# Alternating the small matmuls of an RWKV-7 recurrence over halves of the TensorE array

## The chip, the cores and the metric

The program runs on one core of a Trainium2 chip. The metric is the device time of one execution in microseconds, the median of several runs. Engines are named as the profile names them: PE is TensorE's matmul stream, PEld its weight loads, DVE is VectorE, ACT is ScalarE, POOL is GpSimd, SP is the queue that issues the weight transfers.

## The reference

One layer of a streaming encoder trunk for 256 prompt and 64 sample tokens with the same weights (320 token columns, worked on together):

```python
h = rmsnorm(x, norm_mix)
u_pool, u_rw, g_pool, g_rw = split(h @ w_in)
y_a, new_pool = pool_mixer(u_pool, ...)               # windows 2/4/8/16
y_b, new_shift, S = rwkv7_mix(u_rw, ...)              # 16 heads x 64
merged = sigmoid(g_pool) * (y_a @ proj_pool) + sigmoid(g_rw) * (y_b @ proj_rwkv)
x = x + merged @ w_out
x = x + (silu(h2 @ w_ffn_gate) * (h2 @ w_ffn_up)) @ w_ffn_down
x = x + sigmoid(h3 @ w_ple_gate) * (p @ w_ple_proj)
# inside rwkv7_mix, per token and head:
sa = S @ (-kk_t)
S = S * w_t + outer(sa, b_t) + outer(v_t, k_t)
y = S @ r_t
```

Everything is computed in float32 to float32 accuracy.

## The kernel before

The big products (gemm, L104; mm3, L107) hold features on partitions and stream the 320 token columns. Each weight block is split into a head and a rest in float32r (ACT makes the head, L93; DVE the rest, L56), so a 128 x 128 block costs three matmuls of 320 columns (L110 to L112). There are 11,984 of them in the program, here called gemm matmuls; they accumulate in the two PSUM buffers of tag acc.

The RWKV part works on four groups of four heads (group(g)), with two feature tiles jj of two heads h each. The tokens are cut into five chunks of 64: chunk 4 is the sample, 0 to 3 the prompt. The recurrence is done by chunks, with plain float32 matmuls, each of which stands in the trace as two instructions:

- the decay and in-context rates, tile z: a product with 128 rows (L441), then one with the rest in 64 rows only (L442);
- masked products within a chunk, tiles g0 and g4 (g in the trace, L510 and L513): 64 rows, 128 columns out, 128 moving columns, 20 per group; all of one head half h, then all of the other, because a head half lies on partitions 0 to 63 or 64 to 127;
- two rounds of 32 x 32 products per group for a triangular inverse, pz and px (L569, L574);
- for each chunk in the order 4, 0, 1, 2, 3: a read of the state and of the masked products, ry (L594, L599); an ACT copy, rhs (L603); the solve, pu (L606); an ACT copy, uv (L607); the new state, ps_s (L613), added and scaled by eight small DVE operations on 64 x 64 blocks (L621, L622); the chunk's output, py_c (L628). Chunk 0 starts from no state, chunk 4 from the given one, chunks 1 to 3 from the chunk before.

The order on each engine is made by a scheduler that simulates the program; gemm matmuls of later tiles (the projections of the next group, then as many gate tiles as FILLS says, 5, 4, 4 and 22) are put between the dependent small products. PE takes its instructions in that order. The small products share two PSUM tags of three buffers each:

```python
psB = ctx.enter_context(tc.tile_pool(name="psB", bufs=3, space=PSUM))   # L72
def small(name, shape, tag="pk"):                                       # L82
    return psB.tile(shape, F32, tag=tag, name=name)
```

Of the kernel before, what the change touches and what calls it, by code (L numbers as in the profile page):

```python
# [18 lines left out]
P = 128  # L19
# [20 lines left out]
# columns of the per-feature table  # L40
# [8 lines left out]
def trunk_step(ctx: ExitStack, tc: tile.TileContext, xT, pT, cols, w_low, s0T, poolpast, cst, maskc, invc,  # L49
# [22 lines left out]
    psB = ctx.enter_context(tc.tile_pool(name="psB", bufs=3, space=PSUM))  # L72
# [9 lines left out]
    def small(name, shape, tag="pk"):  # L82
        return psB.tile(shape, F32, tag=tag, name=name)

# [13 lines left out]
    def gemm(acc, src, ks, name, xs, k0=0, first=True, last=True, un=8):  # L98
        """acc += W[k0:k0+ks].T @ x, xs(k) -> (head, rest)"""
# [26 lines left out]
    def rsqrt(pl, v, eps, shape, tag, bufs, out):  # L126
        """out = 1/sqrt(v + eps), with one Newton step"""
# [26 lines left out]
    def shift(q, rp, t, out):  # L154
        """token shift of the projected tile in rp[:, :, 1:]"""
# [6 lines left out]
    # pooling inputs and gates go to DRAM until both branches are projected  # L162
# [20 lines left out]
    # x * g goes to the tensor engine, 1 / rms scales what comes out  # L183
    with tc.tile_pool(name="start", bufs=1) as st:
# [38 lines left out]
        def pp_mm(m0, n, u):  # L223
            h, l = u
            for i in range(n):
                a = small("acc_pp", [P, NT])
# [42 lines left out]
        def narrow(acc, src):  # L269
            """the last low-rank columns come four times: three heads and, in the last rows, the weights' rest"""  # L270
# [39 lines left out]
        zl = rf.tile([P, NT], F32R, name="zl")  # L310
        z_in = []
        for i in range(2):
            lo, hi = slice(64 * i, 64 * i + 64), slice(64 - 64 * i, 128 - 64 * i)
            h = rf.tile([P, NT], F32R, name=f"z{i}")
            act.copy(h[lo], t0[lo])
            act.copy(h[hi], t0[lo])
            TT(zl[lo], t0[lo], f(h[lo]), ALU.subtract)
            z_in.append((lo, h))
# [24 lines left out]
    def pool_diff(gi, z):  # L343
        """trailing means minus the token, split"""
# [22 lines left out]
    def pool_mix(gi, dh, dl):  # L367
        h, l = unit(w_poolw[gi], 4, f"pw{gi}")
        for i in range(2):
            j = 2 * gi + i  # L370
            a = small("acc_pw", [P, NT], "pf")
# [12 lines left out]
    d_gs = dr.tile([8, P, NT], F32, name="d_gs")  # L384
    d_yb = dr.tile([8, P, NT], F32, name="d_yb")
    with tc.tile_pool(name="rk", bufs=1) as rk:

        def shift_tile(q, out):
            """one projected tile with its token shift, into out [P, NT]"""
# [26 lines left out]
        def group(g):  # L416
# [6 lines left out]
            # low-rank paths: decay rate, in-context rate, output gate  # L423
# [20 lines left out]
            go = tp("go")  # L444
            for jj in range(2):
                b = slice((4 + jj) * P, (5 + jj) * P)
                z = small("pg", [P, NT], "pf")
                pe.matmul(out=z, lhsT=lw[:, b], rhs=t1h, start=True, stop=False)
                pe.matmul(out=z, lhsT=lw[:, b], rhs=t1l, start=False, stop=False)
                pe.matmul(out=z, lhsT=lwl[:, jj * P:(jj + 1) * P], rhs=t1h, start=False, stop=False)  # L450
                pe.matmul(out=z, lhsT=lw[0:96, (6 + jj) * P:(7 + jj) * P], rhs=t2s[0:96], start=False, stop=True)
                act.copy(go[:, jj, :], z)
# [12 lines left out]
            # key directions  # L465
# [7 lines left out]
            sqh, sql = split_tp(sq)  # L473
            for jj in range(2):
                s = small("s_kk", [P, NT], "pf")
                head_sum(s, sqh[:, jj, :], sql[:, jj, :])
                vec.tensor_scalar(out=am[:, jj, :], in0=s, scalar1=1e-24, scalar2=None, op0=ALU.max)
# [14 lines left out]
            # r.k bonus  # L492
# [3 lines left out]
            kfh, kfl = split_tp(kf)  # L496
            for jj in range(2):
                s = small("s_rk", [P, NT], "pf")
                head_sum(s, kfh[:, jj, :], kfl[:, jj, :])
                mul(bv[:, jj, :], s, xv[:, jj, :])  # L500
            # masked products within each chunk; rows (b s | k s), columns (a t | r t)
            mg = rk.tile([P, 4, NCH, P], F32, tag="mg", name="mg", bufs=2)
            gm = gmask.unsqueeze(1)
            for h in range(2):
                lo = slice(64 * h, 64 * h + 64)
                g4 = small("g4", [P, 2, P], "pf")
                for jj in range(2):
                    g0 = small("g0", [P, 4, P], "pf")
                    for c in range(4):
                        pe.matmul(out=g0[:, c, :], lhsT=bk[lo, jj, c].rearrange("p s t -> p (s t)"),  # L510
                                  rhs=ar[lo, jj, c].rearrange("p s t -> p (s t)"), start=True, stop=True)
                    mul(mg[:, 2 * jj + h, 0:4, :], g0, gm.broadcast_to([P, 4, P]))
                    pe.matmul(out=g4[:, jj, :], lhsT=bk[lo, jj, 4].rearrange("p s t -> p (s t)"),  # L513
                              rhs=ar[lo, jj, 4].rearrange("p s t -> p (s t)"), start=True, stop=True)
                mul(mg[:, h::2, 4, :], g4, gm.broadcast_to([P, 2, P]))
# [4 lines left out]
            for u0 in range(0, 10, 4):  # L520
                n = min(4, 10 - u0)
                pb = small("pb", [P, n, P], "pf")
# [5 lines left out]
            pv = small("pv", [P, 2, 2, P], "pf")  # L528
            for s in range(2):
                for jj in range(2):  # L530
                    pe.transpose(out=pv[:, s, jj, :], in_=xv[:, jj, s * P:(s + 1) * P], identity=ident)
            pv4 = small("pv4", [64, 2, P], "pf")
            for jj in range(2):
                pe.transpose(out=pv4[:, jj, :], in_=xv[:, jj, 256:320], identity=ident)
            uvf = uv.rearrange("p c h v -> p c (h v)")
            for h in range(2):
                act.copy(uvf[64:128, h:4:2, :], pv[64 * h:64 * h + 64].rearrange("p s j v -> p s (j v)"))
            act.copy(uvf[64:128, 4, :], pv4.rearrange("p j v -> p (j v)"))
            # X = (I - F)^-1, F strictly upper: diagonal blocks by substitution, one block per partition
# [19 lines left out]
            X = rk.tile([64, 20, 64], F32, tag="X", name="X")  # L559
            tz = rk.tile([64, 20, 32], F32, tag="tzz", name="tzz")  # L560
            pool.memset(X[32:64, :, 0:32], 0.0)
            for b in range(2):
                lo = slice(32 * b, 32 * b + 32)
                pool.dma_start(out=X[lo, :, lo], in_=dX[b].rearrange("u s t -> s u t"))
            pool.dma_start(out=tz[0:32], in_=dT.rearrange("u t s -> t u s"))
            for u0 in (0, 10):
                pz = small("pz", [64, 10, 32])
                for u in range(10):
                    pe.matmul(out=pz[32:64, u, :], lhsT=mgu[0:32, u0 + u, 32:64], rhs=tz[0:32, u0 + u, :],  # L569
                              start=True, stop=True)  # L570
                act.copy(tz[32:64, u0:u0 + 10, :], pz[32:64])
                px = small("px", [32, 10, 32])
                for u in range(10):
                    pe.matmul(out=px[:, u, :], lhsT=tz[32:64, u0 + u, :], rhs=X[32:64, u0 + u, 32:64],  # L574
                              start=True, stop=True)
                act.copy(X[0:32, u0:u0 + 10, 32:64], px)
            # chunk recurrence
            ysb = rk.tile([P, 3, 4, C], F32, tag="ysb", name="ysb")
            pool.memset(ysb[64:128, 2], 0.0)
            sbd_in = rk.tile([P, 2, P], F32, tag="sbd", name="sbd_in", bufs=3)  # L580
# [4 lines left out]
            sbd = None  # L585
            for c in (4, 0, 1, 2, 3):
                if c == 4:
                    cur = sbd_in
                elif c == 0:
                    cur = None  # L590
                ry = small("ry", [P, 4, C])
                if cur is not None:
                    for jj in range(2):
                        pe.matmul(out=ry[:, 2 * jj:2 * jj + 2, :].rearrange("p h v -> p (h v)"),  # L594
# [328 lines left out]
```

## Time and profile before

| | |
|---|---|
| median of 3 runs | 1930.12 us (1928.15 to 1931.4) |
| profiled execution, first to last instruction | 1928.3 us |
| PE busy | 1906.9 us, 99% |
| DVE, ACT, POOL busy | 59%, 42%, 7% |
| DMA | 302.98 MB, mean 157 GB/s |

The profile gives no time for the profiled execution other than its span; the median of the runs is 1.8 us above that. Durations of matmul records overlap: a record lasts longer than the distance to the next one, so costs on PE are read from start to start.

### The profile page before, as it was taken

What the parts mean: (1) busy time and instruction counts of PE and PEld (TensorE: products, weight loads), DVE (VectorE), ACT (ScalarE), POOL (GpSimd) and SP (SyncE); (2) the same over time, 40 slices, a digit from 0 to 9 for tenths busy, and PEclk for the clock granted to TensorE, in tenths of its full rate; (3) what the DMA queues carried; (4) which work ended last, traced back from release to release, by engine and by line L of the source; (5) the groups of instructions that cost most, each with busy time, mean ns of one, the idle gap of its engine ahead of it and who ended that gap; (6) DMA issues with size and microseconds to landing.
All of it is one profiled execution on the core that took longest, in us unless ns stands there. A gap on an engine that the chain in (4) does not pass through costs nothing.

```text
span 1928.3 us, 32558 instructions
## 1 busy us (share of the span) xinstructions
PE 1906.9 (99%) x13304; PEld 1873.3 (97%) x13304; DVE 1139.0 (59%) x1764; ACT 803.6 (42%) x1072; POOL 134.7 (7%) x274
## 2 busy tenths in 40 slices
PE   8999999999999999999999999999999999999997
PEld 7999999999999999999999999999999999999997
DVE  7577785788767666555554554444455455444665
ACT  6545436455355334444333333333333333333443
POOL 0101112111031113000000000000000000000000
PEclk9999999999999999999999999999999999999998
DMA  8444444345345566444444444555444444555453
GB/s 280 165 155 154 141 134 150 112 139 189 124 147 178 173 202 233 161 149 149 148 152 152 147 151 144 149 150 158 148 149 153 150 147 149 151 150 151 159 172 119
DMA packets 95221, 302.98 MB, mean 157 GB/s; under 512 B 12096, under 2 KB 23248, under 8 KB 95072
## 3 DMA queue, kind: packets, MB, share of 16 engines
q1 hardware_dynamic: 78336, 271.71, 43.7%
q0 software_dynamic: 6688, 17.39, 3.1%
q10 hardware_dynamic: 10048, 11.80, 1.7%
q8 instruction: 105, 1.72, 0.4%
q14 instruction: 44, 0.36, 0.1%
HBM read 284.12 MB, written 16.73 MB: 156 GB/s over the span
## 4 chain that ended last, share of the span: by engine, by line
PE 98%; DVE 1%; DMA 0%; issue 0%; ACT 0%; DVEq 0%
PE acc_fd L111 5%; PE acc_fg L110 5%; PE acc_fg L112 5%; PE acc_fu L112 5%; PE acc_fu L110 5%; PE acc_fu L111 5%; PE acc_fg L111 5%; PE acc_fd L112 5%; PE acc_fd L110 5%; PE acc_f L112 4%; PE acc_f L111 4%; PE acc_f L110 4%; PE acc_q L110 3%; PE acc_q L112 3%; PE acc_q L111 3%; PE acc_pg L110 2%
## 5 line engine op out<-in xcount | busy, mean ns | idle before, releaser
L111 PE MATMUL acc_fg<-nl,wh_fg 128*128 128x320 f32 x704 | 217.8, 309 | 0.0
L110 PE MATMUL acc_fg<-nh,wh_fg 128*128 128x320 f32 x704 | 217.6, 309 | 0.1
L110 PE MATMUL acc_fu<-nh,wh_fu 128*128 128x320 f32 x704 | 217.5, 309 | 0.0
L112 PE MATMUL acc_fu<-nh,wl_fu 128*128 128x320 f32 x704 | 217.5, 309 | 0.0
L111 PE MATMUL acc_fu<-nl,wh_fu 128*128 128x320 f32 x704 | 217.5, 309 | 0.0
L112 PE MATMUL acc_fg<-nh,wl_fg 128*128 128x320 f32 x704 | 217.5, 309 | 0.0
L56 DVE TENSOR_TENSOR wl_fd<-raw_fd,wh_fd 128x1024 fp32r<-128x1024 f32 (+1 forms) x96 | 109.1, 1136 | 151.7 <-ACT wh_fd L93 151.7
L93 ACT CAST wh_fd<-raw_fd 128x1024 fp32r<-128x1024 f32 (+1 forms) x96 | 94.1, 980 | 203.1 <-PE acc_fd L111 162.4
L93 ACT CAST wh_fg<-raw_fg 128x1024 fp32r<-128x1024 f32 x88 | 92.5, 1051 | 199.4 <-PE acc_fg L111 98.7
L93 ACT CAST wh_fu<-raw_fu 128x1024 fp32r<-128x1024 f32 x88 | 92.5, 1052 | 190.7 <-PE acc_fu L111 100.6
L56 DVE TENSOR_TENSOR wl_fg<-raw_fg,wh_fg 128x1024 fp32r<-128x1024 f32 x88 | 107.8, 1225 | 105.6 <-ACT wh_fg L93 105.6
L110 PE MATMUL acc_f<-xh,wh_f 128*128 128x320 f32 x512 | 160.4, 313 | 0.0
L111 PE MATMUL acc_f<-xl,wh_f 128*128 128x320 f32 x512 | 160.0, 313 | 0.0
L112 PE MATMUL acc_f<-xh,wl_f 128*128 128x320 f32 x512 | 159.8, 312 | 0.1
L110 PE MATMUL acc_fd<-hh,wh_fd 128*128 128x320 f32 x512 | 158.2, 309 | 0.0
L111 PE MATMUL acc_fd<-hl,wh_fd 128*128 128x320 f32 x512 | 158.2, 309 | 0.0
L112 PE MATMUL acc_fd<-hh,wl_fd 128*128 128x320 f32 x512 | 158.2, 309 | 0.0
L56 DVE TENSOR_TENSOR wl_fu<-raw_fu,wh_fu 128x1024 fp32r<-128x1024 f32 x88 | 107.8, 1225 | 83.9 <-ACT wh_fu L93 83.9
L110 PEld LDWEIGHTS acc_fg<-nh,wh_fg 128*128 128x128 f32 x704 | 132.1, 188 | 0.3 <-issue 0.3
L111 PEld LDWEIGHTS acc_fg<-nl,wh_fg 128*128 128x128 f32 x704 | 132.1, 188 | 0.1
L112 PEld LDWEIGHTS acc_fg<-nh,wl_fg 128*128 128x128 f32 x704 | 132.1, 188 | 0.1
L110 PEld LDWEIGHTS acc_fu<-nh,wh_fu 128*128 128x128 f32 x704 | 132.1, 188 | 0.0
(491 smaller groups left out, 5015.3 us busy)
## 6 DMA issues: line engine op xcount, KB each, us to landing
raw_fg<-in_w_gate SPq DMA_DIRECT2D x88, 512.0 KB, 3.7
raw_fu<-in_w_up SPq DMA_DIRECT2D x88, 512.0 KB, 3.8
raw_f<-in_w_in SPq DMA_DIRECT2D x64, 512.0 KB, 4.0
raw_fd<-in_w_down SPq DMA_DIRECT2D x64, 512.0 KB, 3.6
raw_q<-in_w_in SPq DMA_DIRECT2D x48, 512.0 KB, 4.0
raw_o<-in_w_out SPq DMA_DIRECT2D x32, 512.0 KB, 3.8
raw_pg<-in_w_pg SPq DMA_DIRECT2D x32, 512.0 KB, 3.8
raw_fd<-in_w_down SPq DMA_DIRECT2D x32, 384.0 KB, 3.6
```

The source lines that it names most:

```text
L56: return vec.tensor_tensor(out=out, in0=a, in1=b, op=op)
L93: act.copy(h, raw)
L110: pe.matmul(out=acc, lhsT=hs[i], rhs=xh, start=first and i == 0, stop=False)
L111: pe.matmul(out=acc, lhsT=hs[i], rhs=xl, start=False, stop=False)
L112: pe.matmul(out=acc, lhsT=ls[i], rhs=xh, start=False, stop=last and i == n - 1)
```

## The change

The small products are issued in alternation over two parts of the array. Masked products alternate between the row halves h, in two PSUM banks. The inverse's 32 x 32 products for jj = 0 and 1 go to different partitions and alternate. The recurrence keeps jj = 0 on partitions 0 to 63 and jj = 1 on 64 to 127: the read's left side is cut into its two 64-column halves, ra (before the solve) and py_c (after it, where the state is now read a second time), the solve alternates over row halves, and the new state over column halves. Chunks 4 and 0 go through these steps together, so that there are four steps per group and not five. The state update takes four DVE operations of double width. The 64-row product of z is padded with zeros to 128 rows. PSUM tags get one buffer each: s and cs of one bank, w and cw of two banks.

```diff
-    psB = ctx.enter_context(tc.tile_pool(name="psB", bufs=3, space=PSUM))
+    psB = ctx.enter_context(tc.tile_pool(name="psB", bufs=1, space=PSUM))
-    def small(name, shape, tag="pk"):
+    def small(name, shape, tag="s"):
         return psB.tile(shape, F32, tag=tag, name=name)
+    def wide(name, parts=P, tag="w"):
+        return psB.tile([parts, 2, 512], F32, tag=tag, name=name)
...
-                a = small(f"acc_t{q}", [P, NT], "pf")
+                a = small(f"acc_t{q}", [P, NT], ("", "s", "cs")[q])
...
+            zl = rf.tile([P, NT], F32R, name=f"zl{i}")
+            vec.memset(f(zl[hi]), 0.0)
...
-                lo, h = z_in[i]
+                z = wide("z")
                 for jj in range(2):
                     w = lw[:, (2 * i + jj) * P:(2 * i + jj + 1) * P]
-                    z = small("z", [P, NT], "pf")
-                    pe.matmul(out=z, lhsT=w, rhs=h, start=True, stop=False)
-                    pe.matmul(out=z, lhsT=w[lo], rhs=zl[lo], start=False, stop=True)
-                    act.activation(o[:, jj, :], z, AF.Sigmoid, bias=col(c + 2 * g + jj))
+                    for part in range(2):
+                        pe.matmul(out=z[:, jj, 0:NT], lhsT=w, rhs=z_in[i][part], start=part == 0, stop=part == 1)
...
-            for h in range(2):
-                lo = slice(64 * h, 64 * h + 64)
-                g4 = small("g4", [P, 2, P], "pf")
-                for jj in range(2):
-                    g0 = small("g0", [P, 4, P], "pf")
-                    for c in range(4):
-                        pe.matmul(out=g0[:, c, :], lhsT=bk[lo, jj, c]..., rhs=ar[lo, jj, c]..., start=True, stop=True)
+            for jj in range(2):
+                g0 = wide("g0")
+                for c in range(4):
+                    for h in range(2):
+                        product(g0[:, h, c * P:(c + 1) * P], h, jj, c)
...
+            for u in range(10):
+                for jj in range(2):
+                    pe.matmul(out=pz[64 * jj + 32:64 * jj + 64, u, :], lhsT=mgu[0:32, 10 * jj + u, 32:64],
+                              rhs=tz[0:32, 10 * jj + u, :], start=True, stop=True)
...
+            for u in range(10):
+                for jj in range(2):
+                    q = slice(64 * jj + 32, 64 * jj + 64)
+                    pe.matmul(out=px[64 * jj:64 * jj + 32, jj, 32 * u:32 * u + 32], lhsT=tz[q, u, :],
+                              rhs=X[q, u, 32:64], start=True, stop=True)
...
-            for c in (4, 0, 1, 2, 3):
...
+            def read(out, half, c, cur):
+                if cur is not None:
                     for jj in range(2):
+                        pe.matmul(out=out[halves[jj]]..., lhsT=ar[:, jj, c, half, :], rhs=cur[:, jj, :],
+                                  start=True, stop=False)
+                for h in range(2):
+                    for jj in range(2):
+                        pe.matmul(out=out[halves[jj], h, :], lhsT=mg[:, 2 * jj + h, c, halves[half]],
+                                  rhs=uv[:, c, 2 * jj + h, :], start=cur is None and h == 0, stop=h == 1)
+            for cs in ((4, 0), (1,), (2,), (3,)):
+                ra = small("ra", [P, n, 2, C], "cs")
+                for i, c in enumerate(cs):
+                    read(ra[:, i], 0, c, states[c])
+                act.copy(rhs, ra)
+                pu = wide("pu", 64, "cw")
+                for i, c in enumerate(cs):
                     for h in range(2):
+                        for jj in range(2):
+                            pe.matmul(out=pu[:, jj, q:q + C], lhsT=X[halves[jj], h * NCH + c, :],
+                                      rhs=rhs[halves[jj], i, h, :], start=True, stop=True)
...
+                for i, c in enumerate(cs):
+                    for jj in range(2):
+                        for h in range(2):
+                            pe.matmul(out=ps[halves[h], i, jj, :], lhsT=bt[:, jj * NCH + c, halves[h]],
+                                      rhs=uv[:, c, 2 * jj + h, :], start=True, stop=True)
...
+                    for lo in halves:
+                            TT(nxt[lo, :, lo], src, states[c][lo, :, lo], ALU.add)
+                        mul(nxt[lo, :, lo], src, pcs[lo, :, c:c + 1].broadcast_to([64, 2, C]))
...
+                for i, c in enumerate(cs):
+                    read(py[:, i], 1, c, states[c])
```

How the order on PE moves is seen in two places. The first is group 1, chunk 2, late in its recurrence. On PE, before, a read of the state (ry) was followed by masked products of group 2 (g) and by gemm matmuls (acc_f); five rows further on stands the solve pu:

```order
L594 MATMUL ry<-sbd,ar 128x128 x2
L599 MATMUL ry<-uv,mg 64x64 x3
L599 MATMUL ry<-uv,mg 128x64
L510 MATMUL g_3619<-ar,bk 128x128 x4
L110 MATMUL acc_f_5246<-xh,wh_f_0_5249 128x320
L111 MATMUL acc_f_5246<-xl,wh_f_0_5249 128x320
L112 MATMUL acc_f_5246<-xh,wl_f_0_5251 128x320
L110 MATMUL acc_f_5246<-xh,wh_f_0_5249 128x320
L513 MATMUL g_3618<-ar,bk 128x128 x2
```

In the change the same chunk stands on PE like this, with the last gemm matmul ahead of it and the next one behind it:

```order
L117 MATMUL acc_q_4485<-xh,wl_q_8_4520 128x320
L613 MATMUL ra<-sbd,ar 64x128 x2
L617 MATMUL ra<-uv,mg 64x64 x4
L633 MATMUL pu<-rhs,X 64x64 x4
L642 MATMUL ps_s<-uv,bt 64x64 x4
L613 MATMUL py_c<-sbd,ar 64x128 x2
L617 MATMUL py_c<-uv,mg 64x64 x4
L613 MATMUL ra<-sbd,ar 64x128 x2
L617 MATMUL ra<-uv,mg 64x64 x4
L417 MATMUL s_rk<-sp_h,bonesr 128x320
L115 MATMUL acc_q_4554<-xh,wh_q_0_4557 128x320
```

No gemm matmul is left between the read, the solve, the new state and the next chunk's read there. In most of the other steps 20 to 33 gemm matmuls stand between them, as before.

The second place is the masked products of group 0. On PE, before, they came in pieces:

```order
L510 MATMUL g_1120<-ar,bk 128x128 x4
L110 MATMUL acc_q_1873<-xh,wh_q_8_1906 128x320
L111 MATMUL acc_q_1873<-xl,wh_q_8_1906 128x320
L112 MATMUL acc_q_1873<-xh,wl_q_8_1908 128x320
L110 MATMUL acc_q_1873<-xh,wh_q_8_1906 128x320
L513 MATMUL g_1119<-ar,bk 128x128
L510 MATMUL g_1127<-ar,bk 128x128 x4
L513 MATMUL g_1119<-ar,bk 128x128
```

In the change the eight products of one jj stand together on PE, the two head halves in turn:

```order
L117 MATMUL acc_q_1915<-xh,wl_q_8_1950 128x320
L515 MATMUL g_1114<-ar,bk 128x128 x8
L115 MATMUL acc_q_1915<-xh,wh_q_8_1948 128x320
L116 MATMUL acc_q_1915<-xl,wh_q_8_1948 128x320
```

The next such eight follow 29 gemm matmuls later, and the four of chunk 4 another 29 later. Counted over the whole program's PE order, the part of the array that a matmul uses (its rows x columns) changes from one matmul to the next 245 times before and 141 times in the change.

## Rows read from the trace of the kernel before

**Rows 1.** The page: busy time by engine, and the chain that ended last.

```profile
PE 1906.9 (99%) x13304; PEld 1873.3 (97%) x13304; DVE 1139.0 (59%) x1764; ACT 803.6 (42%) x1072; POOL 134.7 (7%) x274
...
PE 98%; DVE 1%; DMA 0%; issue 0%; ACT 0%; DVEq 0%
```

**Rows 2.** Waits of PE (us in total, times, longest), first and last of eight.

```profile
PE acc_pp L110 <- ACT pp L231: 2.5, 3, 1.2
...
PE acc_pp L111 <- DVE pl__125 L56: 0.4, 1, 0.4
```

**Rows 3.** Timeline of PE around one solve: start us, duration us, then the instruction.

```profile
495.51 0.31 PE L110 MATMUL acc_f<-xh,wh_f 128*128 128x320 f32 x1
495.75 0.67 PE L606 MATMUL pu<-rhs,X 64*64 64x64 f32 x8
496.36 0.42 PE L111 MATMUL acc_f<-xl,wh_f 128*128 128x320 f32 x1
496.61 0.31 PE L112 MATMUL acc_f<-xh,wl_f 128*128 128x320 f32 x1
...
499.54 0.31 PE L111 MATMUL acc_f<-xl,wh_f 128*128 128x320 f32 x1
```

**Rows 4.** Timeline of PE around four masked products of one half.

```profile
133.49 0.31 PE L112 MATMUL acc_q<-xh,wl_q 128*128 128x320 f32 x1
133.72 1.16 PE L510 MATMUL g<-ar,bk 64*128 64x128 f32 x8
134.81 0.41 PE L110 MATMUL acc_q<-xh,wh_q 128*128 128x320 f32 x1
135.06 0.30 PE L111 MATMUL acc_q<-xl,wh_q 128*128 128x320 f32 x1
```

**Rows 5.** Groups of PE instructions by line and form: count, busy us, mean ns.

```profile
L510 PE MATMUL g<-ar,bk 64*128 64x128 f32 x128 | 17.4, 281 | 0.0
L606 PE MATMUL pu<-rhs,X 64*64 64x64 f32 x160 | 13.5, 224 | 0.1
```

**Rows 6.** Timeline of PE where products of two array parts meet.

```profile
226.49 0.72 PE L574 MATMUL px<-X,tzz 32*32 32x32 f32 x17
...
227.08 0.19 PE L569 MATMUL pz<-tzz,mg 32*32 32x32 f32 x1
227.08 0.19 PE L574 MATMUL px<-X,tzz 32*32 32x32 f32 x1
...
227.14 0.70 PE L569 MATMUL pz<-tzz,mg 32*32 32x32 f32 x17
...
228.99 0.27 PE L513 MATMUL g<-ar,bk 64*128 64x128 f32 x1
229.10 0.27 PE L510 MATMUL g<-ar,bk 64*128 64x128 f32 x1
229.10 0.27 PE L513 MATMUL g<-ar,bk 64*128 64x128 f32 x1
229.21 0.72 PE L510 MATMUL g<-ar,bk 64*128 64x128 f32 x5
```

**Rows 7.** Timeline of all engines at a hand-off through ACT, group 3.

```profile
586.13 0.59 PE L599 MATMUL ry<-uv,mg 128*64 128x64 f32 x3
...
586.75 0.37 ACT L603 COPY rhs<-ry 128x256 f32<-128x256 f32 x1 [0.49 <-PE ry L599]
...
587.18 0.33 PE L606 MATMUL pu<-rhs,X 64*64 64x64 f32 x2
```

**Rows 8.** The same at the new state's hand-off through DVE.

```profile
591.12 0.61 PE L613 MATMUL ps_s<-uv,bt 128*128 128x128 f32 x4
591.22 1.04 ACT L93 CAST wh_f<-raw_f 128x1024 fp32r<-128x1024 f32 x1 [2.27 <-issue]
591.59 0.98 DVE L56 TENSOR_TENSOR sbd<-ps_s,sbd_in 64x64 f32<-64x64 f32 x4 [1.80 <-PE ps_s L613]
...
593.54 0.82 DVE L622 TENSOR_SCALAR sbd<-sbd,pcs 64x64 f32<-64x64 f32 x3
```

More of the change, by code (lines that the diff above doesn't have):

```diff
@@ L225, in pp_mm @@
             for i in range(n):
-                a = small("acc_pp", [P, NT])
+                tag = ("s", "w", "cs", "cw")[i]
+                a = small("acc_pp", [P, NT], tag) if i % 2 == 0 else wide("acc_pp", tag=tag)[:, 0, 0:NT]
                 mm3(a, [h[:, (2 * i + j) * P:(2 * i + j + 1) * P] for j in range(2)],
@@ new lines, in group, with product @@
+            halves = (slice(0, 64), slice(64, 128))
+            def product(out, h, jj, c):
+                lo = halves[h]
+                pe.matmul(out=out, lhsT=bk[lo, jj, c].rearrange("p s t -> p (s t)"),
+                          rhs=ar[lo, jj, c].rearrange("p s t -> p (s t)"), start=True, stop=True)
+            for jj in range(2):
[3 more added lines that the diff above has]
+                        product(g0[:, h, c * P:(c + 1) * P], h, jj, c)
+                mul(mg[:, 2 * jj:2 * jj + 2, 0:4, :], g0.rearrange("p h (c t) -> p h c t", c=4),
+                    gmask.unsqueeze(1).unsqueeze(1).broadcast_to([P, 2, 4, P]))
@@ L519, in group @@
             bku = bk.rearrange("p j c s t -> p (j c) (s t)")
-            for u0 in range(0, 10, 4):
-                n = min(4, 10 - u0)
-                pb = small("pb", [P, n, P], "pf")
+            for u0, n in ((0, 8), (8, 2)):
+                pb = wide("pb").rearrange("p b (u t) -> p (b u) t", u=4) if n == 8 else small("pb", [P, 2, P])
                 for u in range(n):
@@ L566, in group @@
[L566 to L576, printed above, removed]
@@ L578, in group @@
-            ysb = rk.tile([P, 3, 4, C], F32, tag="ysb", name="ysb")
-            pool.memset(ysb[64:128, 2], 0.0)
-            sbd_in = rk.tile([P, 2, P], F32, tag="sbd", name="sbd_in", bufs=3)
+            X = rk.tile([P, 10, 64], F32, tag="X", name="X")
+            tz = rk.tile([P, 20, 32], F32, tag="tzz", name="tzz")
+            for jj in range(2):
+                pool.memset(X[64 * jj + 32:64 * jj + 64, :, 0:32], 0.0)
+                for b in range(2):
+                    q = 64 * jj + 32 * b
+                    pool.dma_start(out=X[q:q + 32, :, 32 * b:32 * b + 32],
+                                   in_=dX[b, 10 * jj:10 * jj + 10].rearrange("u s t -> s u t"))
@@ new lines, in group @@
+            pool.dma_start(out=tz[0:32], in_=dT.rearrange("u t s -> t u s"))
+            pz = small("pz", [P, 10, 32], "cs")
+            for u in range(10):
[4 more added lines that the diff above has]
+                q = slice(64 * jj + 32, 64 * jj + 64)
+                act.copy(tz[q, 0:10, :], pz[q])
@@ new lines, in group @@
+            px = wide("px", tag="cw")
+            for u in range(10):
+                for jj in range(2):
+                    q = slice(64 * jj + 32, 64 * jj + 64)
+                    pe.matmul(out=px[64 * jj:64 * jj + 32, jj, 32 * u:32 * u + 32], lhsT=tz[q, u, :],
+                              rhs=X[q, u, 32:64], start=True, stop=True)
+            for jj in range(2):
+                q = slice(64 * jj, 64 * jj + 32)
+                act.copy(X[q, :, 32:64], px[q, jj, 0:320].rearrange("p (u t) -> p u t", u=10))
@@ L581, in group @@
+            ysb = rk.tile([P, NCH, 2, C], F32, tag="ysb", name="ysb")
+            sbd_in = rk.tile([P, 2, P], F32, tag="sbd", name="sbd_in", bufs=4)
             pool.memset(sbd_in, 0.0)
@@ L641, in group @@
-            y12 = ysb.rearrange("p s h v -> p (s h) v")
-            st12 = [P, 12]
-            mean = rk.tile(st12, F32, tag="st12", name="mean", bufs=6)
-            vec.tensor_reduce(out=mean, in_=y12, axis=AX.X, op=ALU.add)
+                        pe.matmul(out=out[halves[jj]].rearrange("p h v -> p (h v)"), lhsT=ar[:, jj, c, half, :],
+                                  rhs=cur[:, jj, :], start=True, stop=False)
+                for h in range(2):
+                    for jj in range(2):
+                        pe.matmul(out=out[halves[jj], h, :], lhsT=mg[:, 2 * jj + h, c, halves[half]],
+                                  rhs=uv[:, c, 2 * jj + h, :], start=cur is None and h == 0, stop=h == 1)
@@ new lines, in group @@
+            states = {4: sbd_in, 0: None}
+            for cs in ((4, 0), (1,), (2,), (3,)):
+                n = len(cs)
+                ra = small("ra", [P, n, 2, C], "cs")
+                for i, c in enumerate(cs):
+                    read(ra[:, i], 0, c, states[c])
+                rhs = rk.tile([P, n, 2, C], F32, tag="rhs", name="rhs", bufs=2)
+                act.copy(rhs, ra)
+                pu = wide("pu", 64, "cw")
+                for i, c in enumerate(cs):
+                    for h in range(2):
+                        for jj in range(2):
+                            q = (2 * i + h) * C
+                            pe.matmul(out=pu[:, jj, q:q + C], lhsT=X[halves[jj], h * NCH + c, :],
+                                      rhs=rhs[halves[jj], i, h, :], start=True, stop=True)
+                for i, c in enumerate(cs):
+                    act.copy(uvf[0:64, c, :].rearrange("p (j q) -> p j q", j=2), pu[:, :, i * P:(i + 1) * P])
+                ps = small("ps_s", [P, n, 2, C], "cs")
+                for i, c in enumerate(cs):
+                    for jj in range(2):
+                        for h in range(2):
+                            pe.matmul(out=ps[halves[h], i, jj, :], lhsT=bt[:, jj * NCH + c, halves[h]],
+                                      rhs=uv[:, c, 2 * jj + h, :], start=True, stop=True)
+                new = {}
+                for i, c in enumerate(cs):
+                    nxt = rk.tile([P, 2, P], F32, tag="sbd", name="sbd", bufs=4)
+                    pool.memset(nxt, 0.0)
+                    for lo in halves:
+                        src = ps[lo, i]
+                        if states[c] is not None:
+                            TT(nxt[lo, :, lo], src, states[c][lo, :, lo], ALU.add)
+                            src = nxt[lo, :, lo]
+                        mul(nxt[lo, :, lo], src, pcs[lo, :, c:c + 1].broadcast_to([64, 2, C]))
+                    new[c] = nxt
+                    if c >= 3:
+                        for h, lo in enumerate(halves):
+                            pool.dma_start(out=o_wkv[c - 3, 4 * g + h:4 * g + 4:2].rearrange("j k v -> k j v"),
+                                           in_=nxt[lo, :, lo])
+                py = wide("py_c", tag="cw")[:, 0, 0:n * P].rearrange("p (i h v) -> p i h v", i=n, h=2)
+                for i, c in enumerate(cs):
+                    read(py[:, i], 1, c, states[c])
+                for i, c in enumerate(cs):
+                    act.copy(ysb[:, c], py[:, i])
+                    states[c + 1] = new[c]
@@ L658, in group @@
+            for c in range(NCH):
+                pe.transpose(out=py[:, c * P:(c + 1) * P], in_=ysb[:, c].rearrange("p h v -> p (h v)"), identity=ident)
+            pyj = py[:, 0:NCH * P].rearrange("p (c j t) -> p c j t", c=NCH, j=2)
             for jj in range(2):
                 j = 2 * g + jj
-                py = small("py", [P, NT])
-                for s in range(2):
-                    pe.transpose(out=py[:, s * P:(s + 1) * P], in_=yf[:, s, jj * P:(jj + 1) * P], identity=ident)
-                pe.transpose(out=py[:, 256:320], in_=yf[0:64, 2, jj * P:(jj + 1) * P], identity=ident[0:64, 0:64])
```

134 lines of the change are left out of this document (41 added, 93 removed).

## The prediction

> **What bounds the kernel now.** The page's busy times come first: PE is busy 99% of the span and the chain that ended last is 98% PE [rows 1]. Next, PE's waits: eight entries, 10.6 us together, all in the first 20 us or at the very end [rows 2]. Between about 16 us and the last norm PE never waits for anything that the profile shows. So the time is the sum of what PE issues, and the change is worth what it takes off or adds to that sum, plus any wait that it creates. DVE, ACT and the transfers come in only through such waits.
>
> Busy times of PE can't be added, because matmul records overlap. The timeline from start to start gives the price. Gemm matmuls stand 0.1465 us apart (496.61 to 499.54 is twenty of them) [rows 3]. In the run around pu the next gemm matmul but one starts 1.10 us after the last one before it; two gemm matmuls are 0.29 of that, so eight pu instructions cost 0.81 [rows 3]. The same reading of eight g instructions gives 135.06 - 133.49 - 0.29 = 1.28 us [rows 4]. Each float32 product is two instructions: pu, 80 products, stands there as x160 [rows 5].
>
> What an instruction costs inside such a run: a 32-column px takes (0.72 - 0.19) / 16 = 0.033, and a 128-column g follows the last one of its own half after 0.11 (229.10 to 229.21) [rows 6]; I take 0.032 and 0.112, and for 64 columns 0.058, on the line between. Then pu is 8 x 0.058 = 0.46 of streaming and 0.35 of something else, g 0.90 and 0.38 [rows 3, 4]. The something else is paid for going from the whole array to a part of it and back: the gap before the first small product is 0.24 and the second gemm matmul behind comes late. One change of array part is thus 0.17 to 0.19 us.
>
> **Whether alternation overlaps.** It decides the sign, and the trace shows it by accident. Where the last px met the first pz, which use other rows and other columns, the two start together (227.08 and 227.08), a pair per 0.03 us where one px alone took 0.03 [rows 6]. Where products of the two head halves met, two g instructions started together at 229.10, and the next one at 229.21 [rows 6]. So two instructions on different rows, with the same 128 columns and another PSUM bank, cost the time of one. That is the situation of the changed g and pu, and of px. The changed pz, ra, py_c and ps_s alternate over columns on the same rows, which no row of the trace shows.
>
> **The change part by part, over all four groups.** Streaming before, us: g 160 instructions x 0.112 = 17.9; pu 160 x 0.058 = 9.3; ps_s 80 x 0.112 = 9.0; reads of the state 64 x 0.112 = 7.2; chunk reads in ry and py_c 320 x 0.058 = 18.6; pz and px 320 x 0.032 = 10.2. Together 72.2, less about 0.7 for the places where they already met: 71.5.
>
> After, one behind the other: g 17.9 and pu 9.3 as before; ps_s in 64-column halves 160 x 0.058 = 9.3; the state is now read twice, 128 x 0.112 = 14.3; chunk reads 18.6; pz and px 10.2. Together 79.6. In pairs, half of it: 39.8. Gain 31.7. Its bounds are no overlap at all (a loss of 8.1) and overlap on rows alone, which leaves ps_s, both reads and pz unpaired: 23.6 less gain.
>
> Changes of array part: 245 to 141 by the order, 104 fewer at 0.17 to 0.19 (half of 0.35 and of 0.38), so 18 to 20; I take 18.2. The padding of z is in that: its 64-row product cost no more streaming than a 128-row one, but every one was a way in and out. Fewer steps (16 and not 20) and the products kept together are the rest.
>
> Added at no cost on PE: the two zero halves of zl, set by DVE, which is 59% busy and ahead of PE there; the wider masks and sums on DVE, and double-width state updates in place of eight small ones. The cover is the gemm matmuls between the steps. Where that cover is gone, the hand-off shows:
>
> Through ACT: the last read's record ends at 586.72, the copy takes 0.37, pu starts at 587.18 [rows 7]. Records end some 0.2 after PE could have gone on, so an uncovered hand-off is 0.7 us, and up to 1.04 more when a weight cast is in ACT's way [rows 8]. Through DVE: from the end of ps_s' streaming (591.57) to the last scaling (594.36) it was 2.8, with eight operations and other work between [rows 8]; with four of 0.2 to 0.3, bare, it could be 1.2, and 3.6 behind two weight splits, I take 2.5.
>
> In group 1 the third prompt chunk has none of its cover left (the order's first place): read to solve 0.7 to 1.7, solve to state 0.7 to 1.7, state to the next read 1.2 to 3.6 less 0.4 of py_c, and a little more before it, where sixteen gemm matmuls (2.3 us) stand against a DVE hand-off. Sum 3 to 8; I take 7, since DVE there also works off the next group's elementwise products. In group 3 the last three steps stand 0 to 6 gemm matmuls apart, since the gate tiles that could fill are all behind: two DVE and three ACT hand-offs, less what six matmuls (0.9) cover, 3 to 9; I take 6. At the start, acc_t1 shares its one buffer with the norm's sum ss and waits for the chain that reads it; before it had its own. Bounds 0 to 4; I take 3. What is queued behind each such wait is all of PE, as it issues in order.
>
> Sum: -31.7 - 18.2 + 7 + 6 + 3 = -33.9. Against the profiled execution's span that is 1928.3 to 1894.4; the runs' median lies 1.8 above the span, so **1896 us**.
>
> **The rivals.**
>
> *Column halves don't pair.* Alternation over columns on the same rows would run one behind the other, since nothing in the trace pairs them and the two halves need the same rows' inputs. Then ps_s, reads and pz lose 23.6, PE is slower there, and waits shrink to about 13: -31.7 + 23.6 - 18.2 + 13 = -13.3 gives 1917. For it: only row pairs are seen. Against: px and pz paired with other columns as well, and a pu run on one spot hides each next weight load behind the running matmul (0.058 apart), so loads on the same rows do go ahead. The Trainium skill, page "TensorE: Matmul & The Clock Gate", section "Part 3: Packing small matmuls — row/col tiling", says that weight loads overlap running matmuls only where the row group differs, which speaks for this rival; the same section also gives a 2.38-fold speedup for three column tiles, which speaks against it, and no run here settles it yet. By that first rule the time would be this rival's.
>
> *No pairing at all.* The few pairs in the trace came from a queue that ran dry of the one kind; if strict alternation of two-instruction products pairs nothing, streaming is 8.1 dearer, and 8.1 - 18.2 + 12 = +1.9 gives 1932, no change. The two meetings of different array parts speak against it [rows 6].
>
> *Cover that isn't there.* Slower: one buffer for each tag lets nothing start ahead, so all 48 hand-offs of 16 steps are exposed wherever they outlast the gemm matmuls between, some 22 or 3.2 us. At 1.1 us beyond the cover for each, 53 us are lost: -49.9 + 3 + 53 = +6, 1936. It takes over 1.05 us per hand-off to be slower. Against it: before, hand-offs with the same cover never made PE wait [rows 2].
>
> *Waits smaller than taken.* If ACT and DVE are free at those places, 4 us of waits: 1884.
>
> **How the numbers follow.** The forecast with waits between 10 and 24 us holds 0.62 (own range 1888 to 1904); smaller waits 0.09; larger ones, still faster, up to about 1912, 0.06; columns unpaired 0.14; no pairing 0.04; cover gone 0.05. Range 1885 to 1919 holds the forecast, the larger waits and the column rival. About 0.2% (4 us) is what a measurement of this kernel can tell from no change. Faster 0.91, same 0.04, slower 0.05.
>
> **What would show each step.** Pairs: starts of g two by two, about 0.11 per pair, pu about 0.06, and ra, ps_s, py_c the same if columns pair; one at a time if not. Changes: a gap of 0.24 ahead of a small run and a late second gemm matmul, 141 times and not 245. Waits: PE waiting at ra, pu or ps_s around the third prompt chunk of group 1 and at the end of group 3, and at acc_t1 near 40 us, some 16 us in all. Wrong would be a wait at most steps, or column tiles in single file.

## The result, and the profile after

The change runs in 1900.74 us (median of 4 runs, 1900.61 to 1901.98) against 1930.19 us before (4 runs); the ratio is 0.9849, with a 95% interval of 0.9835 to 0.9863. The profiled execution spans 1898.7 us, 29.6 less than before. The forecast was 1896, from a sum of -33.9; the measured time lies in the range and 4.7 us above the forecast.

The page after, with the busy times and the chain that ended last, answers to [rows 1]:

```profile
PE 1863.8 (98%) x13444; PEld 1838.0 (97%) x13444; DVE 1120.1 (59%) x1674; ACT 798.6 (42%) x1060; POOL 138.7 (7%) x282
...
PE 95%; DVE 3%; DMA 1%; issue 1%; ACT 0%; SPq 0%; DVEq 0%; ACTq 0%
```

PE is still the bound, but 3% of the chain now goes through DVE: there are waits in the middle of the program. Before there were none between 25 us and the last norm. (The prediction's "first 20 us" and "about 16 us" are too early: four of the waits that [rows 2] sums up begin after 16 us, the last of them ends at 24.61. The sum doesn't use them.) These are the waits of PE between 340 and 365 us (the third prompt chunk of group 1), with their total, number and longest:

```profile
PE ra L613 <- DVE sbd L56: 6.4, 2, 4.2
PE pu L633 <- ACT rhs L627: 0.7, 1, 0.7
PE ps_s L642 <- ACT uv L636: 0.5, 1, 0.5
```

and between 540 and 600 us (the end of group 3):

```profile
PE acc_f L115 <- ACT wh_f L98: 1.7, 2, 1.1
PE ra L613 <- DVE sbd L56: 1.7, 2, 1.0
PE ps_s L642 <- ACT uv L636: 0.9, 1, 0.9
PE acc_f L117 <- DVE wl_f L56: 0.8, 1, 0.8
PE acc_pw L115 <- DVE yal L62: 0.5, 1, 0.5
```

That is 7.6 and 5.6 us. The small products themselves are read as before, from the start of the last gemm matmul ahead to that of the second one behind, less 0.29. First a solve, the same eight instructions as in [rows 3]; then sixteen masked products, where [rows 4] has eight; then a read of the state:

```profile
267.90 0.31 PE L117 MATMUL acc_f<-xh,wl_f 128*128 128x320 f32 x1
268.14 0.45 PE L633 MATMUL pu<-rhs,X 64*64 64x64 f32 x8
...
268.78 0.31 PE L116 MATMUL acc_f<-xl,wh_f 128*128 128x320 f32 x1
...
144.64 0.31 PE L117 MATMUL acc_q<-xh,wl_q 128*128 128x320 f32 x1
144.88 1.16 PE L515 MATMUL g<-ar,bk 64*128 64x128 f32 x16
...
146.22 0.31 PE L116 MATMUL acc_q<-xl,wh_q 128*128 128x320 f32 x1
...
264.03 0.31 PE L117 MATMUL acc_f<-xh,wl_f 128*128 128x320 f32 x1
264.27 0.44 PE L613 MATMUL ra<-sbd,ar 128*64 128x128 f32 x4
264.54 0.40 PE L617 MATMUL ra<-uv,mg 128*64 128x64 f32 x8
...
265.12 0.30 PE L116 MATMUL acc_f<-xl,wh_f 128*128 128x320 f32 x1
```

(A line of dots stands for the first gemm matmul behind.) The solve costs 0.59 where it cost 0.81; less 0.35 for the two changes of array part, 0.24 of streaming is left of 0.46. Sixteen g instructions cost 1.29, as much as eight did. The read, whose two halves use all rows and different columns, costs 0.80; four instructions of 128 and eight of 64 columns in single file would be 0.91 and 0.35, in pairs 0.46 and 0.35. All three are in pairs, the column halves too.

The start: the first projection tile of group 0 (acc_q) begins at 47.20 us before and at 50.38 after. First the row of before, then that of the change:

```profile
47.20 0.31 PE L110 MATMUL acc_q<-xh,wh_q 128*128 128x320 f32 x1
```

```profile
50.38 0.31 PE L115 MATMUL acc_q<-xh,wh_q 128*128 128x320 f32 x1
```

One more thing is new. In the table by stretches of group 1's third chunk (start and end, length, busy time of PE, PEld, DVE, ACT, POOL, then the granted clock, the share and rate of the transfers) PE is busy 0.37 of the two us from 346 and 0.87 of the next two, and the granted clock falls to 0.50, the lower of its two levels, for the next ten:

```profile
346.00:348.00 2.00, 0.37 (x9) 0.40 (x11) 1.91 (x6) 1.38 (x2) 1.44 (x3) 1.00 0.79 223
348.00:350.00 2.00, 0.87 (x20) 0.59 (x18) 2.00 (x4) 1.28 (x4) 0.13 (x1) 0.86 0.76 291
350.00:352.00 2.00, 1.43 (x20) 1.24 (x20) 2.00 (x3) 0.27 (x1) 0.00 (x0) 0.50 0.77 250
...
357.00:359.00 2.00, 2.00 (x9) 2.00 (x9) 2.00 (x5) 0.62 (x2) 0.97 (x2) 0.50 0.00 0
```

The same happens behind the waits of group 3:

```profile
578.00:582.00 4.00, 4.00 (x18) 4.00 (x19) 3.65 (x11) 2.64 (x5) 0.00 (x0) 0.57 0.47 154
```

At that level gemm matmuls stand 0.267 apart and not 0.1465. There are 21 of them (from 357.12 and from 578.32), 2.5 us lost; the small products from 349.88 to 356.68 took about 1.3 more than their like elsewhere in the trace. Together some 3.9 us.

### The profile page after: what moved, and what is told of

The parts are those of the page before. It is cut to its first block, busy times and chain, and to the rows that moved or that the text cites. A ratio compares the mean times of both kernels' runs of the same rounds, so it can differ in the third digit from the quotient of the medians.

```text
span 1898.7 us, 32757 instructions
## 1 busy us (share of the span) xinstructions
PE 1863.8 (98%) x13444; PEld 1838.0 (97%) x13444; DVE 1120.1 (59%) x1674; ACT 798.6 (42%) x1060; POOL 138.7 (7%) x282
## 4 chain that ended last, share of the span: by engine, by line
PE 95%; DVE 3%; DMA 1%; issue 1%; ACT 0%; SPq 0%; DVEq 0%; ACTq 0%
PE acc_fd L115 5%; PE acc_fu L116 5%; PE acc_fg L116 5%; PE acc_fg L115 5%; PE acc_fg L117 5%; PE acc_fu L117 5%; PE acc_fd L116 5%; PE acc_fu L115 5%; PE acc_fd L117 5%; PE acc_f L115 4%; PE acc_f L116 4%; PE acc_f L117 4%; PE acc_q L117 3%; PE acc_q L115 3%; PE acc_q L116 3%; PE acc_pg L115 2%
## 5 line engine op out<-in xcount | busy, mean ns | idle before, releaser
L116 PEld LDWEIGHTS acc_fu<-nl,wh_fu 128*128 128x128 f32 x704 | 132.2, 188 | 0.0
```

Source lines behind the costliest of these rows:

```text
L116: pe.matmul(out=acc, lhsT=hs[i], rhs=xl, start=False, stop=False)
```

## The experiments

Each is an edit of the change, unless said otherwise; every kernel computes the whole layer. The change itself stands at 0.9849 of the kernel before. The differences below are between medians; the median of the kernel before moved between 1928.58 and 1930.19 from one set of runs to the next, so a difference of 1 or 2 us says little by itself, and the traces are used beside it. The time at the lower clock is taken from the granted clock in each run's table by stretches: between 60 and 1800 us it is 13.7 us in the change, and PE is busy in 9.0 of them; by the gemm matmuls (0.1465 against 0.267) a busy us at that level loses 0.45.

**1. Every alternation undone.** Each array part gets all its products first.

```diff
-                for c in range(4):
-                    for h in range(2):
+                for h in range(2):
+                    for c in range(4):
                         product(g0[:, h, c * P:(c + 1) * P], h, jj, c)
...
-                    for jj in range(2):
-                        pe.matmul(out=out[halves[jj]]..., rhs=cur[:, jj, :], ...)
-                for h in range(2):
-                    for jj in range(2):
+                for jj in range(2):
+                    if cur is not None:
+                        pe.matmul(out=out[halves[jj]]..., rhs=cur[:, jj, :], ...)
+                    for h in range(2):
                         pe.matmul(out=out[halves[jj], h, :], ...)
```

and likewise in g4, pz, px, pu and ps_s.

> The change with every alternation undone: the same products in the same banks, but each part of the array gets all of its products first and the other part after it. Array-part changes stay at 142 by the order. Theory (pairs come from issuing in alternation, streaming is halved by it): pairs remain only where one part's block meets the next, so 16 to 23 us are lost and the time is 1916 to 1923; the trace shows g one per 0.11 us inside a block. Rival (the gain is that of fewer array-part changes and fewer steps): 1901 or less. Rival (two parts run side by side in whatever order they are issued): 1892 to 1901.

Measured: 1912.08 us, ratio 0.9916 (0.9900 to 0.9933). That is 11.3 above the change, below the theory's 1916 and above both rivals. The trace of this run shows why each was half right. Sixteen g instructions, a solve and a read:

```profile
235.03 0.31 PE L117 MATMUL acc_q<-xh,wl_q 128*128 128x320 f32 x1
235.27 1.71 PE L515 MATMUL g<-ar,bk 64*128 64x128 f32 x16
...
237.16 0.31 PE L116 MATMUL acc_q<-xl,wh_q 128*128 128x320 f32 x1
...
271.63 0.31 PE L117 MATMUL acc_f<-xh,wl_f 128*128 128x320 f32 x1
271.87 0.46 PE L632 MATMUL pu<-rhs,X 64*64 64x64 f32 x8
...
272.50 0.31 PE L116 MATMUL acc_f<-xl,wh_f 128*128 128x320 f32 x1
...
267.48 0.31 PE L117 MATMUL acc_f<-xh,wl_f 128*128 128x320 f32 x1
267.72 0.43 PE L613 MATMUL ra<-sbd,ar 128*64 128x128 f32 x2
267.99 0.22 PE L616 MATMUL ra<-uv,mg 128*64 128x64 f32 x1
267.99 0.32 PE L613 MATMUL ra<-sbd,ar 128*64 128x128 f32 x1
268.04 0.28 PE L616 MATMUL ra<-uv,mg 128*64 128x64 f32 x2
268.15 0.27 PE L613 MATMUL ra<-sbd,ar 128*64 128x128 f32 x1
268.16 0.50 PE L616 MATMUL ra<-uv,mg 128*64 128x64 f32 x5
...
268.84 0.31 PE L116 MATMUL acc_f<-xl,wh_f 128*128 128x320 f32 x1
```

g costs 1.84 and not 1.29, the read 1.07 and not 0.80, but the solve 0.58, no more than with alternation. In the program a half's two state instructions (L613) and its four chunk instructions (L616) come first, and then the six of the other half. In the trace the other half's first L613 starts at 267.99, with the first L616, while three L616 of the half in front have still to start. The two instructions of the first L616 product (267.99 and 268.04) stand on either side of it, which no order of whole products in the program gives. So the other part's work is taken up three instructions early. A block of eight loses five of its eight pairs (0.55 at 0.11), a block of six somewhat over half of what pairing saves (0.27 of 0.45), a block of four nothing. Over the program: 8 runs of g at 0.55, 32 reads at 0.27, 8 runs of pz and px at about 0.53, 17 us; the order of this kernel happens to give group 1's third chunk some cover, and PE's waits between 60 and 1800 us fall from 13.1 to 8.9. That leaves 13. This run is also at the lower clock for less time, 6.8 us (about 356 to 363) and not 13.7:

```profile
360.00:362.00 2.00, 2.00 (x10) 2.00 (x9) 2.00 (x4) 0.56 (x1) 1.17 (x3) 0.50 0.07 29
```

PE is busy in 5.4 of them and not 9.0, which is 1.6 us less lost. Of the 11.5 that this leaves, 11.3 show.

**2. Column alternation alone undone** (both reads, ps_s, pz; the edits are the second part of the diff above).

> Only the alternations over column halves on the same rows are undone (both reads, the new state, pz); g, pu and px still alternate over rows. Theory (column halves pair just as row halves do): 1906 to 1913. Rival that the prediction priced (column halves never pair): nothing is lost in streaming, 1892 to 1901, less than the change because the order at group 1 puts gemm matmuls into the third chunk there.

Measured: 1906.31 us, 0.9882 (0.9867 to 0.9897), 5.6 above the change, with the same 8.9 us of waits as in run 1 and the same 6.8 us at the lower clock. In this run's timeline the read costs 1.06, as in run 1, and not 0.80. Column halves do pair, or undoing their alternation would have cost nothing.

**3. Row alternation alone undone** (g, px, pu).

> Only the alternations over row halves are undone (g, pu, px); the column ones stay. Theory: 1909 to 1915, of which some 4 us are waits at the end of group 3, since its order there gets worse. Rival (the gain lies in fewer changes of array part, 146 here against 141): 1901 to 1903.

Measured: 1907.48 us, 0.9887 (0.9873 to 0.9902), 6.7 above the change. The theory's range was missed by 1.5, and its mechanism holds only in part. Sixteen g instructions cost 1.84 here too, but pu, in blocks of four, lost nothing, as in run 1. The 4 us of waits that were expected on top did not come: PE's waits between 60 and 1800 us fall from 13.1 to 9.9. Against that stands a term that nobody had put in: 20.5 us at the lower clock (350 to 362 and 570 to 580) and not 13.7, some 3 us more lost. The rival is out: the five more changes of array part are 0.9 us of the 6.7.

**4. The padding of z undone.**

```diff
-                        pe.matmul(out=z[:, jj, 0:NT], lhsT=w, rhs=z_in[i][part], ...)
+                        r = slice(64 * i, 64 * i + 64) if part else slice(0, P)
+                        pe.matmul(out=z[:, jj, 0:NT], lhsT=w[r], rhs=z_in[i][part][r], ...)
```

> Only the zero rows of z's second product are taken out again: 64 rows as in the kernel before, same product otherwise. The order has 172 array-part changes and not 141. Theory (0.17 to 0.19 us for each change): 5 to 6 us more, 1906 to 1907. Rival (a change of rows alone, at full column width, costs nothing): 1901.

Measured: 1906.28 us, 0.9881 (0.9866 to 0.9895), 5.5 above the change for 31 more changes of array part: 0.18 us each. The time alone doesn't fix the price so well, since this run has 10.2 us at the lower clock and not 13.7. The rows of z do. First this run, then the change, a product with the rest and the next one:

```profile
316.16 0.41 PE L449 MATMUL z<-zl,lw 64*128 64x320 f32 x1
316.50 0.41 PE L449 MATMUL z<-z,lw 128*128 128x320 f32 x1
```

```profile
392.08 0.31 PE L448 MATMUL z<-zl,lw 128*128 128x320 f32 x1
392.23 0.31 PE L448 MATMUL z<-z,lw 128*128 128x320 f32 x1
```

They stand 0.34 apart here and 0.15 with the padding, 0.19 for a change of array part. The price taken in the prediction holds, for a change of rows at full column width too.

**5. Two gate tiles moved behind group 1.**

```diff
-FILLS = (5, 4, 4, 22)
+FILLS = (5, 6, 4, 20)
```

> The change with two gate tiles moved from behind group 3 to behind group 1 (FILLS 5, 6, 4, 20). Theory (some 9 us of group 1's third chunk and the half clock behind it come from there being no gemm matmul between its steps, and group 3's waits shrink as well): 1887 to 1891, granted clock 1.00 between 340 and 370 us. Rival (the state's hand-off is late because DVE works through the next group's elementwise products, and more cover only moves the wait): 1896 to 1901.

Measured: 1888.60 us, 0.9790 (0.9777 to 0.9804), 12.1 below the change. The stretches that answer to those above show PE busy throughout and the clock at its upper level:

```profile
346.00:348.00 2.00, 2.00 (x16) 2.00 (x15) 1.91 (x6) 1.64 (x3) 1.31 (x3) 1.00 0.87 314
...
350.00:352.00 2.00, 2.00 (x15) 2.00 (x15) 2.00 (x4) 1.05 (x1) 0.00 (x0) 1.00 0.01 1
```

DVE has as much to do there as in the change and PE does not wait for it. So it was cover that was missing, and with it the loss by the clock is gone as well: PE's waits between 60 and 1800 us fall from 13.1 to 6.1, no stretch there is at the lower clock, and these 7.0 and 3.9 us are nearly all of the 12.1. The 6.1 us of waits that are left brought no lower clock.

**6. The same, and other buffers for acc_t1 and acc_t2.**

```diff
-                a = small(f"acc_t{q}", [P, NT], ("", "s", "cs")[q])
+                a = small("acc_t1", [P, NT], "cs") if q == 1 else wide("acc_t2", tag="cw")[:, 0, 0:NT]
```

> As the last, and acc_t1 and acc_t2 get PSUM buffers that the norm's sum ss does not use. Theory (the start loses about 3 us because acc_t1 waits for the chain that reads ss): 2 us below the last, 1885 to 1889. Rival (PE at the start waits for loads and splits anyway): the same as the last within 1 us.

Measured: 1884.81 us, 0.9772 (0.9759 to 0.9786), 3.8 below run 5: more than the 2 of the theory. The first acc_q of group 0 starts where it did in the kernel before:

```profile
47.14 0.31 PE L115 MATMUL acc_q<-xh,wh_q 128*128 128x320 f32 x1
```

PE's waits of the change at the start (0.59 at ss, 1.28 at acc_t2, 0.65 at acc_t1) are gone. Which of the two buffers did it was not separated. This is the fastest kernel of the study, 0.8% below the change.

**7. Chunks 4 and 0 one after the other.**

```diff
-            for cs in ((4, 0), (1,), (2,), (3,)):
+            for cs in ((4,), (0,), (1,), (2,), (3,)):
```

> The change with chunk 4 and chunk 0 one after the other, five steps per group as before (20 and not 16). The order has 158 array-part changes and not 141. Theory: 17 x 0.18 = 3 us for these, and some 4 more of waits in group 1, where the steps stand still closer: 1905 to 1910. Rival (lockstep only shortens chains that are hidden): 1901 to 1904.

Measured: 1906.34 us, 0.9884 (0.9870 to 0.9897), 5.6 above the change, in the theory's range. At 0.18, 17 more changes of array part are 3.1 of it. The rest is not the 4 us of waits that the theory had: they go from 13.1 to 14.1 only. The clock does about as much, with 20.4 us at the lower level (347.0 to 367.4), PE busy in 11.6 of them and not 9.0, 1.2 us more lost.

**8. The kernel before, with FILLS of run 5 alone.**

> The kernel before with FILLS 5, 6, 4, 20 alone. Theory (before, no step lacked cover, so more of it is worth nothing): 1928 to 1931, as before. Rival (the two gate tiles are worth the same in either kernel): 1919 to 1922.

Measured: 1928.68 us, 0.9997 (0.9988 to 1.0006): nothing. The 12 us of run 5 are a loss that the change makes and not a weakness of the old order.

**9. Alternation by blocks of two products,** a test of the reading of run 1.

```diff
-                for c in range(4):
-                    for h in range(2):
+                for c2 in (0, 2):
+                    for h in range(2):
+                        for c in (c2, c2 + 1):
...
```

and likewise, four instructions of one part and then four of the other, in g4, pu, ps_s, pz, px and both reads.

> The change with the two array parts issued in turn by blocks of two products (four instructions) and not product by product, for g, pu, the new state, pz, px and both reads. Theory after the first runs (PE starts the other part's instructions while some three of the block before are still to go, so a block of four is covered whole; blocks of six to twenty lost 0.27 to 0.55 us at each place): no streaming lost, 1896 to 1902, and 16 g instructions in 1.29 us as in the change. Rival (every boundary between blocks leaves a single instruction uncovered, about a third of what the long blocks lost at each of twice as many boundaries): 1905 to 1910, and 16 g instructions in 1.4 to 1.6 us.

Measured: 1901.42 us, 0.9853 (0.9837 to 0.9870): the change's own time. Sixteen masked products in this kernel's timeline:

```profile
143.63 0.31 PE L117 MATMUL acc_q<-xh,wl_q 128*128 128x320 f32 x1
143.87 1.26 PE L515 MATMUL g<-ar,bk 64*128 64x128 f32 x16
...
145.31 0.31 PE L116 MATMUL acc_q<-xl,wh_q 128*128 128x320 f32 x1
```

Sixteen g instructions cost 1.39: 0.10 more than in strict turn, 0.8 us over the eight such runs of the program, and far from the 1.84 of run 1; the reads cost what they do in strict turn. PE's waits between 60 and 1800 us are 10.6 and not 13.1, which pays for it. On g alone the rival's 1.4 is as near as the theory's 1.29; the time is in the theory's range and below the rival's.

**10. One more gate tile each behind groups 0 and 2** (run 6 with FILLS 6, 6, 5, 18).

> As the run with acc_t1's own buffer, with FILLS 6, 6, 5, 18: one more gate tile each behind groups 0 and 2. Theory (what is left of the waits at the end of group 3 comes from the pooling products being due there with too few gate tiles around them): 1882 to 1884. Rival (these waits are DVE's and ACT's own rate on the splits, whatever stands on PE): 1884 to 1887.

Measured: 1885.78 us, 0.9773 (0.9758 to 0.9787), no gain over run 6. The time is in the rival's range, but the rows bear neither out whole. Of PE's waits from 540 to 600 us, 5.0 in run 6, 3.7 are left, and those for the pooling products (acc_pw) fall from 1.4 to 0.5, as the theory had it; but 2.5 us of waits stand between 60 and 540, where run 6 has 0.2, the longest of them 1.6 at pu for rhs. So more tiles do shorten the waits of the pooling products, and the new order loses more elsewhere than that gains.

## Why the prediction was right, step by step

| step | predicted, us | measured, us |
|---|---|---|
| products in pairs | -31.7 | g 0.91, pu 0.24, read 0.45 of streaming, each as priced in pairs |
| 104 changes of array part | -18.2 | 0.18 each (run 4) |
| group 1, third chunk | +7 | waits 7.6 |
| end of group 3 | +6 | waits 5.6, of them 2.6 at hand-offs |
| start, acc_t1 | +3 | 3.2 (50.38 - 47.20) |
| lower clock behind the waits | not in the sum | +3.9 |

*That it is PE's sum* held: run 5 and run 6 move PE's cover and buffers alone and move the time by 12.1 and 3.8, as PE's waits and clock do. The first row's -31.7 as a whole was not measured, only the three prices beside it.

*Pairs on other rows and on other columns* both showed, in the trace of the change and by runs 2 and 3. The rival that column halves don't pair (1917) is out. The Trainium skill, page "TensorE: Matmul & The Clock Gate", section "Part 3: Packing small matmuls — row/col tiling", says that weight loads overlap running matmuls only where the row group differs; the read above, with both halves on all 128 rows, streams in 0.45 where single file would be 0.91, and its twelve weight loads stand between 264.27 and 264.80, while its matmuls run, so here the measurement decides against that sentence, and for the speedup by column tiles in the same section. That section also says that matmuls start strictly in the program's order; run 1 shows matmuls of the other array part starting ahead of three that stand before them.

*That alternation makes the pairs* was too strong. The prediction read the meeting of px and pz [rows 6] as an accident of the order; it was the rule at work. The other part's products need to be next in line, not alternate with these: blocks of four instructions do almost as well (run 9). What alternation itself is worth is what run 1 takes away, by the prices read there some 17 of the 39.8 us of streaming that pairs save; by the same account the other 23 come from putting the halves on two array parts next to each other at all.

*No pairing at all* (1932) and *cover that isn't there* at 1.05 us per hand-off (1936) are out: between 60 and 1800 us PE waits at 7 of the 48 hand-offs (4 times for sbd, twice for uv, once for rhs), all of them where the forecast put them or just ahead.

*The waits* were sized almost exactly in sum, and that is in part luck. At the end of group 3 the forecast counted hand-offs of the recurrence; they are 2.6 of the 5.6 (1.7 for sbd, 0.9 for uv), and the other 3.0 are gemm matmuls that wait for their weight splits (acc_f) and for the pooling products (acc_pw), which it did not have. At the start the wait at acc_t1 itself is 0.65; the rest of the 3.2 is mostly the waits at ss and acc_t2 (run 6). In group 1 one part left its bounds: state to next read was put at 1.2 to 3.6 us. The rows of DVE there:

```profile
351.27 0.82 DVE L56 TENSOR_TENSOR bk<-kf,pinv 128x640 f32<-128x640 f32 x1
352.12 0.61 DVE L56 TENSOR_TENSOR sbd<-ps_s,sbd 64x128 f32<-64x128 f32 x2
...
353.96 1.01 DVE L62 SCALAR_TENSOR_TENSOR kf<-xr,ct,kf 128x320 f32<-128x320 f32 x2
354.89 0.60 DVE L56 TENSOR_TENSOR sbd<-sbd,pcs 64x128 f32<-64x128 f32 x2
...
355.63 0.69 PE L613 MATMUL ra<-sbd,ar 128*64 128x128 f32 x4 [4.20 <-DVE sbd L56]
```

The new state's sums are added at 352.12 and scaled at 354.89, with the next group's elementwise products ahead of them and between; from the end of ps_s' streaming (350.36) to the last scaling (355.49) it is 5.1 us. Other parts of that chunk were shorter than taken. Whether the scaling alone, put next to its sum, would have been enough was not tried.

*The step that was missing* is the clock: the sum took every wait at its own length. Behind the two longest groups of waits PE went on at half speed, and that is most of the 4.3 us by which the difference of the spans (-29.6) falls short of the forecast's sum (-33.9). With it the sum is -49.9 + 7.6 + 5.6 + 3.2 + 3.9 = -29.6, the difference of the spans. That it comes out to the tenth is luck: the kernel before had a stretch at the lower clock of its own (below), worth 1.5, which the sum doesn't hold, so about as much stays unexplained.

## What to carry to other kernels

Where small matmuls use half of the array, place the two halves' products on different array parts, rows or columns, and next to each other in the program; blocks of four instructions do almost as well as strict turns. Each change of array part costs 0.18 us here by itself, so a half-array product between full ones is worth padding with zeros when its streaming is the same. When such a change shortens PE's work, look at once for the steps that lose their cover: a wait of PE costs its own length and, behind the longest ones here, a stretch at the lower clock as well (the 5 to 6 us of waits in runs 5 and 6 brought none), and moving two independent tiles there was worth 12 us, two fifths as much again as the change.

## What the runs showed of the hardware that had not been expected

The part of the array that comes next is started up to three instructions early, past instructions of the part in front (run 1): three of a block of six, as the read's rows show.

The lower clock does not need a wait. In the kernel before, the table by stretches shows it at 322 us, with PE busy all the time; what stood ahead, from 317.67 to 321.5, were small and partial products (py, pz, z):

```profile
322.00:324.00 2.00, 2.00 (x10) 2.00 (x9) 1.55 (x3) 0.17 (x1) 1.13 (x2) 0.57 0.79 225
324.00:326.00 2.00, 2.00 (x10) 2.00 (x9) 0.00 (x0) 0.00 (x0) 0.00 (x0) 0.58 0.97 308
```

Twelve gemm matmuls stand 0.267 apart there, 1.5 us. The change has no such stretch at that place. Nor does the kernel before bring it each time: in run 8 the same products stand from 314.43 to 318.29, and the granted clock is 1.00 from 314 to 326.
